# z and v projected in 512 columns for four token blocks at once, and the scan's decay tiles issued early

## The chip, the cores and the metric

The kernel runs on one core of a Trainium2 chip. The metric is the device time of one execution in microseconds (us). The engines of the core are TensorE (PE in the profile; its weight loads, which overlap the matmuls, are listed apart as PEld), VectorE (DVE), ScalarE (ACT), GpSimd (POOL) and SyncE (SP, whose queue issues the transfers). They run side by side, each in its own order, and wait for one another by semaphores.

## The reference

One layer of a decoder for one sequence of 512 tokens and 1024 features, all in float32: half a SwiGLU feed-forward, a mixer, and another half SwiGLU feed-forward, each added to x. The mixer projects the normed x once and gives the columns to two groups of heads. Cut to what matters here:

```python
proj = h @ w_in[l]                               # h = rms_norm(x), (512, 1024)
z, xbc, dt_raw, q, k, v = jnp.split(proj, split_idx, axis=-1)
xbc = jax.nn.silu(causal_dwconv(xbc, conv_w[l], conv_b[l]))
xs, bm, cm = jnp.split(xbc, [SSD_WIDTH, SSD_WIDTH + SSD_GROUPS * SSD_STATE], axis=-1)
...
a_cs = jnp.cumsum(dt * a.reshape(g, hg), axis=2)             # within a chunk of 128 tokens
xdt = xs * dt[..., None]
seg = a_cs[:, :, :, None] - a_cs[:, :, None, :]
decay = jnp.where(causal, jnp.exp(jnp.where(causal, seg, 0.0)), 0.0)
cb = jnp.einsum("bcign,bcjgn->bcijg", cm, bm)
y_diag = jnp.einsum("bcijgh,bcjghp->bcighp", cb[..., None] * decay, xdt)
... # states handed from chunk to chunk
y = y_diag + y_off + xs * d_skip
...
gated = (y_ssd * jax.nn.silu(z)).reshape(bsz, s, SSD_GROUPS, SSD_WIDTH // SSD_GROUPS)
y_ssd = rms_norm(gated, ssd_norm_w).reshape(bsz, s, SSD_WIDTH)
o = diff_attention(q, k, v, lam)                 # and a norm per head
x = x + concat([y_ssd, o]) @ w_out[l]
```

z and v are 1024 columns wide each; the scan has two groups of eight heads and four chunks of 128 tokens.

## The kernel before, in words

**The products.** Every float32 product of a projection is made of three matmuls: both operands are split into a high and a low part, and high x high, high x low and low x high are added up in PSUM, the memory into which PE writes. The normed x lies as `nm.xh` and `nm.xl` with the features on the partitions, in eight contraction blocks (`KD`) of 128.

**The weights.** They come in a fixed list of pieces of 128 x 1024 (`mixp`, L83 on). SP loads a piece into one of three `raw` tiles (`load_raw`), ACT casts it to the high part `whi` (L109), DVE subtracts to get the low part `wlo` (L110). `piece()` hands over the next one and has two more prepared ahead.

**The stages.** The first feed-forward takes until about 350 us. Then the columns xbc are projected and convolved (to about 440): `conv_tile` ends with a Silu on ACT (L467), `conv_tr` turns each result to tokens on the partitions with four transposes (`xt`, L474) and a copy (L476). Then come z and v, interleaved with the scan (440 to 570), then q and k with the attention (to about 755), the output projection and the second feed-forward.

**z and v before.** `tok_proj` projects 256 columns at a time: it takes two pieces of four contraction blocks, and for each of the four token blocks j runs 24 matmuls of 256 columns (lines L592 to L594). Two token blocks share one PSUM bank, from the pool behind `pJ`. It is a generator that yields after each token block; such a part is a unit. When a half is done, `cb` empties the bank. For z that is (`hr` holds half of the norm's factor of each token)

```python
S.activation(th, ps[:, jj, :], AF.Tanh, scale=hr[:, j:j + 1])
S.activation(zr, ps[:, jj, :], AF.Copy, scale=hr[:, j:j + 1])
V.scalar_tensor_tensor(zr, th, 1.0, zr, op0=ALU.add, op1=ALU.mult)
```

which is silu(z) = h (1 + tanh h) with h = z/2, on lines L608 to L610; for v it is a scaled copy (L617).

**The scan.** It has eight steps (c, g). `ssd_a` prepares one: a broadcast load of the decay sums from DRAM into the tile `ab` (L628), the product `cb` on PE and its masked copy `cbm` on DVE, then on ACT eight Relus (L634) and one Exp over 1024 columns (L635), on DVE `xdt`, the product `ab` x `cbm` (L639) and `xdd`, and on ACT eight scaled slices for `y` (L646). `ssd_o` takes the state on (L658 to L667), `ssd_d` makes the diagonal products `pd` (L676: eight matmuls of plain float32, each of which the profile shows as two) and multiplies with `sz`. `ssd_n` norms a group over its four chunks (L690), `ssd_c` transposes the result (`yt`, L697) and stores it. The tiles `ab`, `cbm`, `xdt` and `y` come from a pool `sb`, which is opened after the convolution's pool was closed and lies in the same memory.

**What sets the order.** A scheduler of the framework decides in which order each engine gets its instructions, from the program's order and its own estimates; the loop over the steps calls `unit()` between the parts of the scan, which is how projection lands between them. ScalarE loads a table of functions (L635 ACT_TABLE_LOAD) when the next function isn't in the table it holds; Silu and Exp are not in the same one here.

Of the kernel before, what the change touches and what calls it, by code (L numbers as in the profile page):

```python
# [8 lines left out]
F32 = mybir.dt.float32  # L9
# [3 lines left out]
AF = mybir.ActivationFunctionType  # L13
ALU = mybir.AluOpType
# [4 lines left out]
P = 128  # L19
T = 512  # L20
NB = T // P
KD = 8
# [16 lines left out]
def hymba_layer(ctx: ExitStack, tc: tile.TileContext, xT, gu1, dn1, wxbc, wdt, wz, wv, wqk,  # L39
                wo, gu2, dn2, cols, rows, out):  # L40
    nc = tc.nc
    V, S, G, PE = nc.vector, nc.scalar, nc.gpsimd, nc.tensor
# [6 lines left out]
    def pM(name, dt=F32):  # L49
        return pspool.tile([P, T], dt, tag="P", name=name)  # L50

    pJ = pP = pM
# [31 lines left out]
    mixp = [(wxbc[t], 1024) for t in (8, 9, 10, 11)]  # L84
    mixp += [(wdt, 128)]
    mixp += [(wxbc[t], 1024) for t in range(8)]
    for w, g in ((wz, 0), (wz, 1), (wv, 0), (wz, 2), (wz, 3), (wv, 1), (wv, 2), (wv, 3)):
        mixp += [(w[g, i], 1024) for i in range(2)]
    mixp += [(wqk[h, i], 1024) for h in range(8) for i in range(2)]
    for ds in ((0, 1), (2, 3), (4, 5)):  # L90
        mixp += [(wo[d, 0], 1024) for d in ds] + [(wo[d, 1, :, 0:512], 512) for d in ds]
# [7 lines left out]

    def load_raw(src, n):  # L100
        raw = wpool.tile([P, 1024], F32, tag="raw", name="raw", bufs=3)
        nc.sync.dma_start(raw[:, :n], src)
        return raw

    def split_part(raw, hi, lo, a, b):
# [14 lines left out]
    def prep(upto):  # L120
        while len(ready) < min(upto, len(pieces)):
            i = len(ready)
            if pieces[i][0] == "plain":
                _, src, n = pieces[i]
                ready.append(split_w(load_raw(src, n), n))
                continue
            r1, r2 = load_raw(pieces[i][1], 1024), load_raw(pieces[i][2], 1024)
            b11, b21, b12, b22 = r1[:, :512], r1[:, 512:], r2[:, :512], r2[:, 512:]
            n = scratch["n"]
            t = scratch["t"][:, n % 2] if n > 1 else scratch["hp"].tile([P, 2048], F32, tag="hp", name="tw0")  # L130
            scratch["n"] += 1
            t1, t3, t2, t4 = (t[:, q * 512:(q + 1) * 512] for q in range(4))
            V.tensor_sub(t1, b12, b11)
            V.tensor_sub(t3, b22, b12)
            V.tensor_sub(t2, b22, t1)
            V.tensor_sub(t4, t2, b21)
            ready.append([split_w(r1, 1024), split_w(t[:, :1024], 1024), split_w(t[:, 1024:], 1024),
                          split_w(b22, 512)])

    def piece(ahead=2):  # L140
        i = taken[0]
        taken[0] += 1
        prep(i + 1 + ahead)
        return ready[i]

    def blk(w, k, width=P):
        return w[:, k * width:(k + 1) * width]
# [25 lines left out]
    triu = const.tile([P, P], F32, name="triu")  # L173
# [219 lines left out]
    nm = [None]  # L393
# [8 lines left out]
    nm = nm[0]  # L402
# [7 lines left out]
    vt = [mix.tile([P, NB, 256], F32, tag=f"v{g}", name=f"v{g}") for g in range(4)]  # L410
# [22 lines left out]
    ssd = ssd_cm.__enter__()  # L433
    xs = ssd.tile([P, NB, 1024], F32, name="xs")
    sz = ssd.tile([P, NB, 1024], F32, name="sz")
    bT = ssd.tile([P, 2, T], F32, name="bT")
    cT = ssd.tile([P, 2, T], F32, name="cT")
    btok = ssd.tile([P, NB, 2, P], F32, name="btok")
    dts = ssd.tile([P, NB, 16], F32, name="dts")
    acs = ssd.tile([P, NB, 16], F32, name="acs")  # L440
# [3 lines left out]
    acs_d = dram.tile([64, P], F32, name="acs_d")  # L444
# [99 lines left out]
    for n, pair in enumerate(order):  # L544
# [3 lines left out]
        ps = [pP(f"xbc{n}{i}") for i in range(2)]  # L548
# [9 lines left out]
        for i in range(2):  # L558
            w = piece()
# [14 lines left out]
    hr = const.tile([P, NB], F32, name="hr")  # L574
# [4 lines left out]
    def tok_proj(name, cb, ahead=2):  # L579

        ws = [piece(ahead), piece(ahead)]
        for half in range(2):
            ps = pJ(f"{name}_{half}")
            psv = ps.rearrange("p (b c) -> p b c", c=256)
            for jj in range(2):
                j = half * 2 + jj
                o = psv[:, jj, :]
                for k in range(KD):
                    w = ws[k // 4]
                    hi, lo = blk(w[0], k % 4, 256), blk(w[1], k % 4, 256)  # L590
                    xh, xl = nm.xh[:, k, j * P:(j + 1) * P], nm.xl[:, k, j * P:(j + 1) * P]
                    PE.matmul(o, lhsT=xh, rhs=hi, start=k == 0, stop=False)  # L592
                    PE.matmul(o, lhsT=xh, rhs=lo, start=False, stop=False)  # L593
                    PE.matmul(o, lhsT=xl, rhs=hi, start=False, stop=k == KD - 1)  # L594
                if jj == 1:
                    cb(half, psv)
                yield
# [1 line left out]
    state = ssd.tile([P, 2, T], F32, name="state")  # L599
    sview = lambda a: a.rearrange("p (a b) -> p a b", b=64)  # L600

    def z_group(g):
        def cb(half, ps):
            for jj in range(2):
                j = half * 2 + jj
                zr = sz[:, j, g * 256:(g + 1) * 256]
                th = sb.tile([P, 256], F32, tag="th", name="th")
                S.activation(th, ps[:, jj, :], AF.Tanh, scale=hr[:, j:j + 1])  # L608
                S.activation(zr, ps[:, jj, :], AF.Copy, scale=hr[:, j:j + 1])
                V.scalar_tensor_tensor(zr, th, 1.0, zr, op0=ALU.add, op1=ALU.mult)  # L610
        return tok_proj(f"z{g}", cb)

    def v_group(g):
        def cb(half, ps):
            for jj in range(2):
                j = half * 2 + jj
                S.activation(vt[g][:, j, :], ps[:, jj, :], AF.Copy, scale=nm.r[:, j:j + 1])  # L617
        return tok_proj(f"v{g}", cb)

    ssq = [ssd.tile([P, NB], F32, name=f"ssq{g}") for g in range(2)]  # L620

    def ssd_a(c, g):

        hs = slice(g * 8, g * 8 + 8)
        sh = [P, 8, 64]
        cs = slice(c * P, (c + 1) * P)
        ab = sb.tile([P, 8, P], F32, tag="ab", name="ab", bufs=3)
        nc.sync.dma_start(ab, acs_d[c * 16 + g * 8:c * 16 + g * 8 + 8, :].partition_broadcast(P))  # L628
        pcb = pM(f"cb{c}{g}")
        PE.matmul(pcb[:, :P], lhsT=bT[:, g, cs], rhs=cT[:, g, cs], start=True, stop=True)  # L630
        cbm = sb.tile([P, P], F32, tag="cbm", name="cbm")
        V.tensor_mul(cbm, pcb[:, :P], triu)
        for h in range(8):
            S.activation(ab[:, h, :], ab[:, h, :], AF.Relu, bias=acs[:, c, g * 8 + h:g * 8 + h + 1], scale=-1.0)  # L634
        S.activation(ab, ab, AF.Exp, scale=-1.0)  # L635
        xg = sview(xs[:, c, g * 512:(g + 1) * 512])
        xdt = sb.tile(sh, F32, tag="xdt", name="xdt")
        V.tensor_tensor(xdt, xg, dts[:, c, hs].unsqueeze(2).to_broadcast(sh), op=ALU.mult)
        V.tensor_tensor(ab, ab, cbm.unsqueeze(1).to_broadcast([P, 8, P]), op=ALU.mult)  # L639
        xdd = None  # L640
        if c < NB - 1:
            xdd = sb.tile(sh, F32, tag="xdd", name="xdd", bufs=1)
            V.tensor_tensor(xdd, xdt, dsd[:, c, hs].unsqueeze(2).to_broadcast(sh), op=ALU.mult)
        y = sb.tile(sh, F32, tag="y", name="y")
        for h in range(8):
            S.activation(y[:, h, :], xg[:, h, :], AF.Copy, scale=row[:, R_DS + g * 8 + h:R_DS + g * 8 + h + 1])  # L646
        return ab, xdt, xdd, y

# [50 lines left out]
        nc.sync.dma_start(ysave[:, g * 4:g * 4 + 4, c, :], yt)  # L699

    steps = [(c, g) for g in range(2) for c in range(NB)]
    units = [z_group(0), z_group(1), v_group(0), z_group(2), z_group(3), v_group(1), v_group(2), v_group(3)]

    def unit(n=1):

        while n and units:
            try:
                next(units[0])
                n -= 1
            except StopIteration:  # L710
                units.pop(0)

    unit()
    for t, dst in last_conv:
        conv_tr(t, dst)
# [2 lines left out]
    sb = sb_cm.__enter__()  # L718
    unit()
    ops = ssd_a(*steps[0])  # L720
    unit(2)
    for n, s in enumerate(steps):
        ssd_o(*s, *ops)
        unit()
        nxt = ssd_a(*steps[n + 1]) if n < 7 else None
        unit()
        ssd_d(*s, *ops)
        ops = nxt
        if s[0] == NB - 1:
            ssd_n(s[1])  # L730
        if n in (5, 6):
            for c in (0, 1) if n == 5 else (2, 3):
                ssd_c(c, 0)
        unit()
# [324 lines left out]
```

## Time and profile before

| what | value |
|---|---|
| median of 3 runs | 1178.77 us (1178.4 to 1179.59) |
| own time of the profiled execution | 1178.91 us |
| its span in the profile | 1177.2 us |
| mean granted clock of PE over the span | 0.993 |
| PE busy | 1163.6 us |
| DVE busy | 854.4 us |
| ACT busy | 546.0 us |

All rows of this document are from that one profiled execution; its own time is 1.7 us more than its span, since the span begins with the first recorded instruction. A start in the rows is in us from there. Matmuls overlap in the engine, so the time that one of them costs is read from the distance of two starts, not from its own duration.

### The profile page before, as it was taken

How to read it: one execution, taken by the hardware profiler on the slowest of the kernel's cores; microseconds unless marked ns; L12 is line 12 of the kernel's file. 1: busy time of each engine (PE TensorE's matmuls, PEld its weight loads, DVE VectorE, ACT ScalarE, POOL GpSimd, SP SyncE). 2: the span in 40 equal slices, each digit the busy share in tenths (PEclk: the TensorE clock that was granted, in tenths of full speed). 3: DMA queues.
4: the chain of work that ended last, by engine and by line, in shares of the span. 5: the costliest groups of instructions: out<-in, count | busy, mean ns of one | idle time of the engine just before them, and what ended most of it. 6: DMA issues, size and time to landing. Idle time of an engine off the chain costs nothing.

```text
span 1177.2 us, 18641 instructions
## 1 busy us (share of the span) xinstructions
PE 1163.6 (99%) x7435; PEld 1026.4 (87%) x7435; DVE 854.4 (73%) x1509; ACT 546.0 (46%) x938; POOL 36.0 (3%) x63
## 2 busy tenths in 40 slices
PE   8999999999999998999999999999999999999998
PEld 6789999999888788999988887688889999999986
DVE  6887877877768974685477877436798888777763
ACT  5443343433344458794465656334354443334331
POOL 1000000000013000000000000013000000000000
PEclk9999999999999998999999999899999999999999
DMA  7323333333245223323421204144222333333332
GB/s 234 90 64 98 94 102 109 112 95 112 79 134 197 73 89 126 108 83 112 130 73 36 67 25 130 33 161 127 71 79 92 115 114 95 103 108 99 105 103 85
DMA packets 42391, 119.53 MB, mean 102 GB/s; under 512 B 4608, under 2 KB 9920, under 8 KB 42304
## 3 DMA queue, kind: packets, MB, share of 16 engines
q1 hardware_dynamic: 41024, 114.15, 31.6%
q0 software_dynamic: 1280, 4.20, 1.0%
q8 instruction: 58, 0.95, 0.3%
q14 instruction: 29, 0.24, 0.1%
HBM read 112.00 MB, written 6.32 MB: 101 GB/s over the span
## 4 chain that ended last, share of the span: by engine, by line
PE 97%; ACT 1%; DMA 0%; DVE 0%; SPq 0%; issue 0%; POOL 0%
PE s L308 10%; PE s L306 10%; PE s L307 10%; PE dn L153 7%; PE dn L152 7%; PE dn L151 7%; PE gu L151 3%; PE gu L152 3%; PE gu L153 3%; PE qk L592 3%; PE wo L151 3%; PE wo L152 3%; PE wo L153 3%; PE qk L594 3%; PE qk L593 3%; PE sc L801 2%
## 5 line engine op out<-in xcount | busy, mean ns | idle before, releaser
L109 ACT CAST whi<-raw 128x1024 fp32r<-128x1024 f32 (+2 forms) x217 | 189.5, 875 | 316.9 <-PE s L307 123.1
L110 DVE TENSOR_TENSOR wlo<-raw,whi 128x1024 fp32r<-128x1024 f32 (+3 forms) x225 | 223.0, 993 | 127.6 <-ACT whi L109 121.7
L307 PE MATMUL s<-al,whi 128*128 128x256 f32 x952 | 266.4, 281 | 0.0
L306 PE MATMUL s<-ah,whi 128*128 128x256 f32 x952 | 265.4, 281 | 0.0
L308 PE MATMUL s<-ah,wlo 128*128 128x256 f32 x952 | 264.8, 281 | 0.0
L307 PEld LDWEIGHTS s<-al,whi 128*128 128x128 f32 x952 | 179.3, 188 | 2.2
L306 PEld LDWEIGHTS s<-ah,whi 128*128 128x128 f32 x952 | 178.8, 188 | 2.3
L308 PEld LDWEIGHTS s<-ah,wlo 128*128 128x128 f32 x952 | 178.3, 188 | 0.1
L152 PE MATMUL dn<-h,whi 128*128 128x512 f32 x352 | 139.0, 395 | 0.0
L153 PE MATMUL dn<-h,wlo 128*128 128x512 f32 x352 | 138.7, 395 | 0.0
L151 PE MATMUL dn<-h,whi 128*128 128x512 f32 x352 | 137.9, 395 | 0.0
L109 ACT CAST whi<-tw 128x1024 fp32r<-128x1024 f32 x68 | 70.3, 1050 | 144.0 <-PE s L307 64.9
L110 DVE TENSOR_TENSOR wlo<-tw,whi 128x1024 fp32r<-128x1024 f32 x68 | 81.9, 1217 | 3.0 <-ACT whi L109 2.9
L153 PEld LDWEIGHTS dn<-h,wlo 128*128 128x128 f32 x352 | 66.1, 188 | 15.0
L151 PEld LDWEIGHTS dn<-h,whi 128*128 128x128 f32 x352 | 66.1, 188 | 14.3
L152 PEld LDWEIGHTS dn<-h,whi 128*128 128x128 f32 x352 | 66.2, 188 | 13.7
L592 PE MATMUL qk<-whi,xhm 128*128 128x256 f32 x256 | 74.2, 290 | 0.0
L594 PE MATMUL qk<-whi,xlm 128*128 128x256 f32 x256 | 71.9, 281 | 0.0
L593 PE MATMUL qk<-wlo,xhm 128*128 128x256 f32 x256 | 71.7, 280 | 0.0
L342 DVE SCALAR_TENSOR_TENSOR x<-dn,x 128x512 f32<-128x512 f32 x64 | 44.0, 687 | 37.3 <-PE dn L153 36.3
L151 PE MATMUL gu<-xh,whi 128*128 128x512 f32 x160 | 64.9, 406 | 2.1 <-POOL whi L107 2.0
L152 PE MATMUL gu<-xl,whi 128*128 128x512 f32 x160 | 63.6, 398 | 0.0
(274 smaller groups left out, 2248.9 us busy)
## 6 DMA issues: line engine op xcount, KB each, us to landing
raw<-in_gu SPq DMA_DIRECT2D x86, 512.0 KB, 3.6
raw<-in_dn SPq DMA_DIRECT2D x48, 384.0 KB, 3.2
raw<-in_wqk SPq DMA_DIRECT2D x16, 512.0 KB, 3.6
raw<-in_wxbc SPq DMA_DIRECT2D x12, 512.0 KB, 3.7
raw<-in_wo SPq DMA_DIRECT2D x10, 512.0 KB, 3.7
raw<-in_dn SPq DMA_DIRECT2D x16, 256.0 KB, 2.7
raw<-in_wz SPq DMA_DIRECT2D x8, 512.0 KB, 3.6
raw<-in_wv SPq DMA_DIRECT2D x8, 512.0 KB, 3.6
```

What stands on the lines that cost most here:

```text
L109: S.copy(hi[:, a:b], raw[:, a:b])
L110: V.tensor_sub(lo[:, a:b], raw[:, a:b], hi[:, a:b].bitcast(F32))
L151: PE.matmul(ps, lhsT=hi, rhs=xh, start=start, stop=False)
L152: PE.matmul(ps, lhsT=hi, rhs=xl, start=False, stop=False)
L153: PE.matmul(ps, lhsT=lo, rhs=xh, start=False, stop=stop)
L306: PE.matmul(ps, lhsT=hi, rhs=ah[:, i, a], start=i == 0, stop=False)
L307: PE.matmul(ps, lhsT=hi, rhs=al[:, i, a], start=False, stop=False)
L308: PE.matmul(ps, lhsT=lo, rhs=ah[:, i, a], start=False, stop=i == 3)
L342: V.scalar_tensor_tensor(x[d], ps, 0.5, x[d], op0=ALU.mult, op1=ALU.add)
L592: PE.matmul(o, lhsT=xh, rhs=hi, start=k == 0, stop=False)
L593: PE.matmul(o, lhsT=xh, rhs=lo, start=False, stop=False)
L594: PE.matmul(o, lhsT=xl, rhs=hi, start=False, stop=k == KD - 1)
```

## The change

Four things change in the stretch from about 440 to 570 us.

*Wider groups.* `tok_pair` takes the place of `tok_proj` for z and v: a matmul has 512 columns, two groups of 256. A piece now holds two contraction blocks of both groups, so its `raw` tile is filled by two transfers of 256 KB, and the operand of a matmul is two runs of 256 columns, 512 apart. All four token blocks are worked on with each piece, in four PSUM banks that are held from the first piece to the fourth. q and k still use `tok_proj`.

*z's activation.* The Tanh is written in place into PSUM; Copy goes first, and DVE reads the Tanh from PSUM. The tile `th` is gone.

*The decay tile.* `ssd_ab` is cut out of `ssd_a`; `ab` and `cbm` come from the longer-lived pool `ssd`, and the first decay tile is issued ahead of the first unit. The exp table is loaded by an instruction of its own ahead of that.

*ScalarE's order.* `tc.issue_after` pins the Relus and the Exp of each decay tile behind the Exp of the one before (the first behind the table load), and the slices for `y` behind the Exp of their own step.

```diff
@@ -84,8 +84,9 @@
-    for w, g in ((wz, 0), (wz, 1), (wv, 0), (wz, 2), (wz, 3), (wv, 1), (wv, 2), (wv, 3)):
-        mixp += [(w[g, i], 1024) for i in range(2)]
+    for w in (wz, wv):
+        for g in (0, 2):
+            mixp += [(tuple(w[g + b, i, :, c:c + 512] for b in range(2)), 1024) for i in range(2) for c in (0, 512)]
...
@@ -99,7 +100,10 @@
-        nc.sync.dma_start(raw[:, :n], src)
+        parts = src if isinstance(src, tuple) else (src,)
+        m = n // len(parts)
+        for q, part in enumerate(parts):
+            nc.sync.dma_start(raw[:, q * m:(q + 1) * m], part)
...
@@ -599,50 +603,78 @@
-    def z_group(g):
...
-    def v_group(g):
...
+    def tok_pair(name, cb):
+
+        ps = [None] * NB
+        for q in range(4):
+            w = [z.rearrange("p (g k c) -> p k g c", g=2, k=2) for z in piece()]
+            for half in range(2):
+                for j in (2 * half, 2 * half + 1):
+                    if q == 0:
+                        ps[j] = pJ(f"{name}_{j}")
+                    o = ps[j].rearrange("p (g c) -> p g c", g=2)
+                    for kk in range(2):
+                        k = 2 * q + kk
+                        xh, xl = nm.xh[:, k, j * P:(j + 1) * P], nm.xl[:, k, j * P:(j + 1) * P]
+                        PE.matmul(o, lhsT=xh, rhs=w[0][:, kk], start=k == 0, stop=False)
+                        PE.matmul(o, lhsT=xh, rhs=w[1][:, kk], start=False, stop=False)
+                        PE.matmul(o, lhsT=xl, rhs=w[0][:, kk], start=False, stop=k == KD - 1)
+                    if q == 3:
+                        cb(j, ps[j])
+                yield
+
+    def z_pair(g):
+        def cb(j, ps):
+            zr = sz[:, j, g * 512:(g + 1) * 512]
+            S.activation(zr, ps, AF.Copy, scale=hr[:, j:j + 1])
+            S.activation(ps, ps, AF.Tanh, scale=hr[:, j:j + 1])
+            V.scalar_tensor_tensor(zr, ps, 1.0, zr, op0=ALU.add, op1=ALU.mult)
+        return tok_pair(f"z{g}", cb)
+
+    def v_pair(g):
+        def cb(j, ps):
+            for b in range(2):
+                S.activation(vt[2 * g + b][:, j, :], ps[:, b * 256:(b + 1) * 256], AF.Copy, scale=nm.r[:, j:j + 1])
+        return tok_pair(f"v{g}", cb)
...
+    def ssd_ab(c, g):
+
+        cs = slice(c * P, (c + 1) * P)
+        ab = ssd.tile([P, 8, P], F32, tag="ab", name="ab", bufs=3)
+        nc.sync.dma_start(ab, acs_d[c * 16 + g * 8:c * 16 + g * 8 + 8, :].partition_broadcast(P))
...
+        cbm = cbms[c, g] = ssd.tile([P, P], F32, tag="cbm", name="cbm", bufs=2)
+        V.tensor_mul(cbm, pcb[:, :P], triu)
+        with tc.issue_after(pinned[0]):
+            for h in range(8):
+                S.activation(ab[:, h, :], ab[:, h, :], AF.Relu, bias=acs[:, c, g * 8 + h:g * 8 + h + 1], scale=-1.0)
+            e = S.activation(ab, ab, AF.Exp, scale=-1.0)
+        pinned[0] = e.ins
+        return ab, e.ins
 
     def ssd_a(c, g):
...
+        ab, y_after = abs_.pop((c, g)) if (c, g) in abs_ else ssd_ab(c, g)
...
+        with tc.issue_after(y_after):
+          for h in range(8):
             S.activation(y[:, h, :], xg[:, h, :], AF.Copy, scale=row[:, R_DS + g * 8 + h:R_DS + g * 8 + h + 1])
         return ab, xdt, xdd, y
...
@@ -699,7 +731,7 @@
-    units = [z_group(0), z_group(1), v_group(0), z_group(2), z_group(3), v_group(1), v_group(2), v_group(3)]
+    units = [z_pair(0), z_pair(1), v_pair(0), v_pair(1)]
...
@@ -710,6 +742,8 @@
+    pinned[0] = tc.keep_in_program_order(S.preload_act_table_set("exp_and_others")).ins
+    abs_[steps[0]] = ssd_ab(*steps[0])
     unit()
...
@@ -718,7 +752,7 @@
     unit()
     ops = ssd_a(*steps[0])
-    unit(2)
+    unit(4)
```

The scheduler turns this into the following orders; numbers at a name tell one buffer from another.

ScalarE between the convolution and the first Exp, before. `ab_4241` is the first decay tile, `ab_4368` the second, `y_` the slices, `th_` and `sz_` belong to z, `whi_` is a weight cast:

```order
L634 ACTIVATE ab_4241<-ab_4241,acs_3495 128x128 x8
L109 CAST whi_4333<-raw_4331 128x1024
L634 ACTIVATE ab_4368<-ab_4368,acs_3495 128x128 x3
L608 ACTIVATE th_4319<-z0_1_4270,hr_4149 128x256
L609 ACTIVATE sz_3490<-z0_1_4270,hr_4149 128x256
L608 ACTIVATE th_4323<-z0_1_4270,hr_4149 128x256
L609 ACTIVATE sz_3490<-z0_1_4270,hr_4149 128x256
L667 COPY state_4153<-st00_4328 128x512
L109 CAST whi_4339<-raw_4337 128x1024
L634 ACTIVATE ab_4368<-ab_4368,acs_3495 128x128 x3
L635 ACT_TABLE_LOAD
L635 ACTIVATE ab_4241<-ab_4241 128x1024
```

ScalarE in the changed kernel, from the convolution's last Silu (L471) on. `ab_4159` is the first decay tile, `ab_4330` the second, `xt6` and `xt7` the last two transposes of the convolution:

```order
L471 ACTIVATE xst_4149<-a_4144 128x512
L745 ACT_TABLE_LOAD
L656 ACTIVATE ab_4159<-ab_4159,acs_3495 128x128 x8
L480 COPY xs_3489<-xt6_4195 128x4x128
L657 ACTIVATE ab_4159<-ab_4159 128x1024
L656 ACTIVATE ab_4330<-ab_4330,acs_3495 128x128 x8
L480 COPY xs_3489<-xt7_4201 128x4x128
L678 ACTIVATE y_4230<-xs_3489,row_3476 128x64 x8
L113 CAST whi_4273<-raw_4270 128x1024
L657 ACTIVATE ab_4330<-ab_4330 128x1024
L678 ACTIVATE y_4350<-xs_3489,row_3476 128x64 x8
L656 ACTIVATE ab_4433<-ab_4433,acs_3495 128x128
```

The table load, the Relus and the Exp of the first tile now stand directly behind the last Silu, and the slices for `y` behind the Exp of their step. Before, the first Exp stood behind z's activations and parts of the second tile's Relus.

The queue of SP, before. `acs_d` is the DRAM copy of the decay sums, the loads on L628 fill the decay tiles, those on L102 the weight pieces:

```order
L540 DMA acs_d_3499<-acsT_3926 64x128
L102 DMA raw_4162<-in_wz 128x1024
L102 DMA raw_4331<-in_wv 128x1024
L102 DMA raw_4337<-in_wv 128x1024
L102 DMA raw_4536<-in_wz 128x1024
L628 DMA ab_4241<-acs_d_3499 128x1024
L628 DMA ab_4368<-acs_d_3499 128x1024
```

and in the changed kernel:

```order
L106 DMA raw_4174<-in_wz 128x512 x2
L544 DMA acs_d_3499<-acsT_3926 64x128
L649 DMA ab_4159<-acs_d_3499 128x1024
L649 DMA ab_4330<-acs_d_3499 128x1024
L649 DMA ab_4433<-acs_d_3499 128x1024
L106 DMA raw_4239<-in_wz 128x512 x2
```

The three decay loads (now L649) moved up past three pieces of v and one of z, to a place right behind the store.

PE at the first `pd`, in the changed kernel (L708). `z0_3` is the fourth token block of the first pair, `z1_0` the first of the second pair:

```order
L619 MATMUL z0_3_4218<-whi_4242,xhm_3280 128x512
L620 MATMUL z0_3_4218<-wlo_4243,xhm_3280 128x512
L621 MATMUL z0_3_4218<-whi_4242,xlm_3281 128x512
L708 MATMUL pd000_4301<-xdt_4225,ab_4159 128x64 x8
L619 MATMUL z1_0_4395<-whi_4273,xhm_3280 128x512
L620 MATMUL z1_0_4395<-wlo_4274,xhm_3280 128x512
L621 MATMUL z1_0_4395<-whi_4273,xlm_3281 128x512
L619 MATMUL z1_0_4395<-whi_4273,xhm_3280 128x512
L620 MATMUL z1_0_4395<-wlo_4274,xhm_3280 128x512
L621 MATMUL z1_0_4395<-whi_4273,xlm_3281 128x512
L619 MATMUL z1_1_4402<-whi_4273,xhm_3280 128x512
```

The bank of `z1_1` is the second that the next pair asks for, six matmuls behind the eight of `pd`. Before, `pd` stood behind 144 matmuls of 256 columns, now behind 96 of 512.

## Rows read from the trace of the kernel before

**Rows 1.** The page's part 1: busy us, share of the span, instructions.

```profile
PE 1163.6 (99%) x7435; PEld 1026.4 (87%) x7435; DVE 854.4 (73%) x1509; ACT 546.0 (46%) x938; POOL 36.0 (3%) x63
```

**Rows 2.** The waits of PE, whole run: us in total, times, longest.

```profile
PE pd L676 <- DVE ab L639: 4.7, 1, 4.7
...
PE at L825 <- DVE nmx L808: 1.2, 1, 1.2
```

**Rows 3.** Windows: length, busy us of PE to POOL, PE clock, DMA share, GB/s.

```profile
450.00:500.00 50.00, 45.31 (x331) 42.23 (x330) 28.61 (x41) 39.88 (x108) 0.00 (x0) 0.93 0.36 113
700.00:750.00 50.00, 48.80 (x276) 36.40 (x275) 34.79 (x93) 30.11 (x72) 0.00 (x0) 0.94 0.29 90
```

**Rows 4.** A window of 4 us, the same columns.

```profile
464.00:468.00 4.00, 4.00 (x21) 4.00 (x22) 1.78 (x4) 4.00 (x12) 0.00 (x0) 0.54 0.00 0
```

**Rows 5.** The timeline of PE: start, duration, instruction, [idle before, releaser].

```profile
458.85 0.28 PE L594 MATMUL z<-whi,xlm 128*128 128x256 f32 x1
463.82 3.21 PE L676 MATMUL pd<-xdt,ab 128*128 128x64 f32 x16 [4.69 <-DVE ab L639]
466.79 0.56 PE L592 MATMUL z<-whi,xhm 128*128 128x256 f32 x1
...
471.20 0.28 PE L594 MATMUL z<-whi,xlm 128*128 128x256 f32 x1
...
479.25 1.89 PE L676 MATMUL pd<-xdt,ab 128*128 128x64 f32 x16
480.95 0.36 PE L592 MATMUL v<-whi,xhm 128*128 128x256 f32 x1
481.15 0.28 PE L593 MATMUL v<-wlo,xhm 128*128 128x256 f32 x1
```

**Rows 6.** The chain that ended last, 446 to 475: start, us, what.

```profile
448.68 2.64 ACT y L646 x12
...
452.42 2.16 ACT ab L634 x7
454.57 0.94 ACT whi L109
...
456.40 0.36 ACT th L608
...
457.84 0.47 ACT state L667
...
460.16 1.28 ACT L635
461.45 1.06 ACT ab L635
462.54 1.24 DVE ab L639
```

**Rows 7.** The waits of SP's queue, 420 to 610.

```profile
SPq L628 <- PE xt L474: 4.6, 1, 4.6
```

**Rows 8.** The timeline of ACT at the convolution's last Silu.

```profile
444.44 0.64 ACT L467 ACTIVATE xst<-a 128x512 f32<-128x512 f32 x1
```

**Rows 9.** The timeline of PE: xbc (46 steps) and z (27 steps).

```profile
428.10 0.40 PE L152 MATMUL xbc<-xlm,whi 128*128 128x512 f32 x1
...
438.83 0.39 PE L153 MATMUL xbc<-xhm,wlo 128*128 128x512 f32 x1
...
440.05 0.28 PE L593 MATMUL z<-wlo,xhm 128*128 128x256 f32 x1
...
443.20 0.28 PE L593 MATMUL z<-wlo,xhm 128*128 128x256 f32 x1
```

**Rows 10.** The page's part 5: group | busy, mean ns | idle before.

```profile
L342 DVE SCALAR_TENSOR_TENSOR x<-dn,x 128x512 f32<-128x512 f32 x64 | 44.0, 687 | 37.3 <-PE dn L153 36.3
```

**Rows 11.** The timelines of DVE and PE at the end of the scan.

```profile
560.28 2.74 DVE L690 SCALAR_TENSOR_TENSOR sz<-sz,ssr,row 128x512 f32<-128x512 f32 x4
...
569.61 0.60 PE L697 MATMUL yt<-ident,sz 128*128 128x128 f32 x4
```

More of the change, by code (lines that the diff above doesn't have):

```diff
@@ L600, in hymba_layer @@
     sview = lambda a: a.rearrange("p (a b) -> p a b", b=64)
-    def z_group(g):
[L603 to L611, printed above, removed]
@@ L613, in v_group @@
-    def v_group(g):
[L614 to L618, printed above, removed]
-    ssq = [ssd.tile([P, NB], F32, name=f"ssq{g}") for g in range(2)]
+    def tok_pair(name, cb):
[16 more added lines that the diff above has]
+                yield
@@ new lines, in hymba_layer @@
+    ssq = [ssd.tile([P, NB], F32, name=f"ssq{g}") for g in range(2)]
+    abs_, cbms = {}, {}
+    pinned = [None]
+    def ssd_ab(c, g):
+        cs = slice(c * P, (c + 1) * P)
+        ab = ssd.tile([P, 8, P], F32, tag="ab", name="ab", bufs=3)
+        nc.sync.dma_start(ab, acs_d[c * 16 + g * 8:c * 16 + g * 8 + 8, :].partition_broadcast(P))
+        pcb = pM(f"cb{c}{g}")
+        PE.matmul(pcb[:, :P], lhsT=bT[:, g, cs], rhs=cT[:, g, cs], start=True, stop=True)
+        cbm = cbms[c, g] = ssd.tile([P, P], F32, tag="cbm", name="cbm", bufs=2)
[6 more added lines that the diff above has]
+        return ab, e.ins
@@ L626, in ssd_a @@
         cs = slice(c * P, (c + 1) * P)
[L627 to L635, printed above, removed]
+        ab, y_after = abs_.pop((c, g)) if (c, g) in abs_ else ssd_ab(c, g)
         xg = sview(xs[:, c, g * 512:(g + 1) * 512])
@@ L638, in ssd_a @@
         V.tensor_tensor(xdt, xg, dts[:, c, hs].unsqueeze(2).to_broadcast(sh), op=ALU.mult)
-        V.tensor_tensor(ab, ab, cbm.unsqueeze(1).to_broadcast([P, 8, P]), op=ALU.mult)
+        V.tensor_tensor(ab, ab, cbms.pop((c, g)).unsqueeze(1).to_broadcast([P, 8, P]), op=ALU.mult)
         xdd = None
@@ L644, in ssd_a @@
         y = sb.tile(sh, F32, tag="y", name="y")
-        for h in range(8):
+        with tc.issue_after(y_after):
+          for h in range(8):
             S.activation(y[:, h, :], xg[:, h, :], AF.Copy, scale=row[:, R_DS + g * 8 + h:R_DS + g * 8 + h + 1])
```

## The prediction

> **What bounds the kernel now.** I read the page's busy shares first: TensorE (PE) is busy 1163.6 of 1177.2 us [rows 1]. Only two things can then make the kernel faster: less time per matmul, or the few microseconds in which PE waits or runs at its lower clock. The waits of PE come next. The longest in the whole run is 4.7 us, by the diagonal products `pd` of the scan (L676), for the product `ab` of VectorE (DVE); near the end of attention there is one of 1.2 us [rows 2]. The windows of 50 us say the same and add the clock: the one from 450 has 45.31 busy us at a mean granted clock of 0.93, the one from 700 a clock of 0.94 [rows 3]. A finer window shows what follows the idle: from 464 to 468 PE is busy all the time, at 0.54, so most of it runs at the lower of its two levels, 1.2 GHz [rows 4].
>
> What the stall costs comes from the starts of PE's instructions [rows 5]. The last z matmul before it starts at 458.85 and `pd` at 463.82, 4.97 apart, where a 256-column matmul holds PE for 0.1167 (below): 4.85 lost. After it the eight `pd` products take 463.82 to 466.79 = 2.97 us, the next chunk's 479.25 to 480.95 = 1.70: 1.27 lost. Then 20 steps of 256-column matmuls take 466.79 to 471.20 = 4.41 us; at full clock they are 20 x 0.1167 (below) and 0.08 more for the first behind `pd`, which starts its successor after 0.20 in the next chunk, so 2.42: 1.99 lost. **Stall and slow stretch together: 4.85 + 1.27 + 1.99 = 8.11 us.**
>
> Why `pd` waited is in the chain that ended last [rows 6]. From 448.7 to 462.5 it lies on ScalarE (ACT), which hardly idles there: it scales fifteen slices for `y`, only then begins the Relus of the first decay tile, weaves in casts, Relus of the next tile, z's activations and the state copy, and at 460.16 loads the exp table (1.28) for the first Exp; DVE's product follows, and PE starts. Part of it begins earlier: the SP queue held the decay loads for 4.6 us, behind the convolution's last transposes `xt`, which still read the memory where the decay tiles lie [rows 7].
>
> **The change, part by part.**
>
> *The first decay tile is early.* Its tiles now live in the long-lived pool; the order of the SP queue puts the three loads right behind the store of `acs`, ahead of the fourth z piece. ACT issues table load, eight Relus and Exp directly behind the convolution's last Silu, which before ran 444.44 to 445.08 [rows 8]; with 0.3 for the `cbm` product now ahead of it on DVE (my guess), 445.4. Prices from the chain [rows 6]: load 1.28, a Relu 2.16/7 = 0.31, an Exp 1.06, and for the copy that stands between them, 512 columns out of PSUM, the state copy's 0.47. Exp of step 0 ends at 445.4 + 1.28 + 2.47 + 0.47 + 1.06 = 450.7. DVE then needs its small products and the 1.24 of `ab` [rows 6]: about 453.
>
> When does PE ask for it? Before, from the second z matmul at 440.05 [rows 9] to one spacing after the last at 458.85 [rows 5] lay 143 of 256 columns, 16.7 us, and 2.2 us of transposes, state product and `cb`. Now 96 of 512 columns stand there, 22.4 us, and the same 2.2: `pd` comes due at about 464.6, with its input ready since 453. The 11 us between are what hides this edit; were they gone, each us that the tile is late would be paid again. The stall and its slow stretch go: **-8.11 us.**
>
> *512 columns instead of 256.* 768 matmuls become 384. The 512-column convolution projection starts one each (438.83 - 428.10)/46 = 0.2333 us, z's 256-column ones (443.20 - 440.05)/27 = 0.1167 [rows 9]: twice the latter is the former. Starts are printed to 0.01, so at most 1 ns per matmul can hide in that, 0.4 us in all; I take 0. The operand is now two runs of 256 columns, which no row has. Bounds: one run of 512 at 0.2333, and two whole matmuls of 256, also 0.2333; I take 0 again.
>
> The Trainium skill, page "TensorE: Matmul & The Clock Gate", section "Back-to-back issue gap", gives a warm matmul a fixed 2.5 ns beside its columns. By it the 384 fewer would save 0.96 us (an estimate from that page), and the sum would be -9.1; the rows just read do not show that part.
>
> *Four token blocks at once, two contraction blocks a piece.* Each piece still serves 24 x 0.2333 = 5.6 us of PE, as before. But a pair now keeps four PSUM banks until its end, so the next pair's banks come free only through ACT and DVE. This is where a stall could arise next, so I followed ACT to there. Behind 450.7, by the chain's prices [rows 6]: eight Relus 2.47, copy 0.47, eight `y` slices at 2.64/12 = 0.22, 1.76, a cast 0.94, Exp 1.06, `y` 1.76, Relus with two casts 4.35, state copy 0.47: 464.0. Then Copy and Tanh of block 0, 512 columns each. No row has them in place in PSUM; the state copy of 512 from PSUM takes 0.47, two of the old 256-column ones 2 x 0.36 = 0.72. I take 0.47, the same width: 464.9; DVE's scalar_tensor_tensor from PSUM, 0.69 [rows 10], makes 465.6. PE asks for the second bank of the next pair after `pd` (1.70) and six matmuls (1.40): 467.7. Margin 2.1 us, or 1.6 with the dearer end. The later boundaries have more: the next z drains start behind an idle ACT (it waits there for decay loads whose buffer the `pd` two steps earlier frees), and v's drains have one operation less per column. Queued behind such a wait on ACT are casts for pieces that PE needs over 15 us later, so it costs nothing; with that cover gone it would cost one for one.
>
> The page "ScalarE: Activation LUTs" of the Trainium skill, section "What ACT_TABLE_LOAD costs", adds a drain of 1.38 us to each switch; here the Exp starts 0.01 after the load of 1.28 ends [rows 6], so the trace does not show it. By that page the margin would be 0.7 (an estimate), still no stall.
>
> *The rest.* SP issues 16 more loads of half the size, hidden in a queue that waits for free buffers. ACT does 16 operations of 0.47 for z in place of 32 of 0.36, DVE 8 of 0.69 for 16 smaller ones; neither bounds. Between the last `pd` and the last transposes `yt` PE has 144 matmuls of 256 columns before, 16.8 us, and now 36 wide and 24 narrow ones, 11.2 us, so `yt` is asked for 5.6 us sooner after `pd`. What it needs first, the first of four norm products, was done at 560.28 + 2.74/4 = 560.97, 8.6 us before it was asked for at 569.61 [rows 11]. Cover 3.0 us: cost 0.
>
> **Sum:** own time of the profiled execution 1178.91 - 8.11 = 1170.80. That execution stands 0.14 above the median of 1178.77, so I forecast 1170.7 us.
>
> **Rivals.**
> 1. *The bank wait appears.* ACT is later than worked out by more than the 1.6 to 2.1 of margin, and PE waits at the first boundary. For: ACT is loaded without a gap for 20 us, and the added Tanh in place is unseen. Against: all other prices are rows. Idle of 1 to 4 us at full clock: 1171.7 to 1174.7.
> 2. *The same wait, longer: not faster.* If ACT's order holds the drains back so far that PE idles and its clock falls as at 464, the price is the idle and 1.27 + 1.99 = 3.26; from 4.85 us of idle on, ACT being 6.5 to 7.0 us late, nothing is gained, and with 9 us of idle the time is 1170.7 + 9 + 3.26 = 1183.
> 3. *Two runs cost more than one.* From 8.11/384 = 21 ns per matmul on it eats the gain; at 40 ns the time is 1186. The Trainium skill's page "PSUM — Partial Sum Buffer", section "Specifications (TRN2)", says non-contiguous access slows matmuls significantly; the output here is contiguous, only the moving operand is not. Against it: two whole 256-column matmuls already cost no more than one of 512 [rows 9].
> 4. *The other slow stretch changes.* A clock of 0.94 over 50 us costs 3.0 us [rows 3]. The wait there is only 1.2 us [rows 2]; with the scan ending earlier, it may fall differently: 1167.7.
> 5. *Matmuls do have a fixed part* beside their columns: up to 0.4 us by the rows, 1170.3. The page on TensorE would give 1169.7 by its 2.5 ns.
>
> **How the numbers follow.** Forecast (1170.7, give or take 1) 0.62; rival 1 0.15; rival 2 0.06; rival 3 0.04; rival 4 0.08; rival 5 0.05. A difference under 0.2% (2.4 us) cannot be told from none here: faster means below 1176.4. The cases but rivals 2 and 3 lie there, less 0.01 of rival 1: 0.89 faster. Rivals 2 and 3 begin at no gain, and with that 0.01 give 0.05 same and 0.06 slower. The range takes in rivals 4 and 1: 1167.3 to 1175.3, leaving out about 0.12. The likeliest case alone: 1169.7 to 1171.7.
>
> **What would show it.** PE's wait by `pd` for `ab` is gone, and the window from 450 has 50 busy us at clock 1.00. The 512-column z matmuls start every 0.2333 us. The last scan transposes, at 569.61 before [rows 11], start at about 561.5. ACT's Copy and Tanh of block 0 start near 464, and PE waits for no `sz`. Attention, from there on, looks as before, 8.1 us earlier. I am wrong if the first z matmuls of the second pair wait for DVE or ACT, if their spacing is over 0.24, or if the gain by 569 is lost again by 800.

## The result and the profile after

The changed kernel takes 1168.78 us in the median (1167.5 to 1173.2 over four runs), the kernel before 1178.63 us in the same comparison; the ratio is 0.9925 with an interval of 0.9911 to 0.9939, so 7 to 10.5 us less. The forecast was 1170.7 us. The profiled execution took 1168.65 us at a span of 1166.9, 10.3 us less than the span of before.

The page's part 1 of the kernel after, in the order of [rows 1]:

```profile
PE 1158.3 (99%) x7051; PEld 1004.0 (86%) x7051; DVE 854.2 (73%) x1501; ACT 543.5 (47%) x922; POOL 36.1 (3%) x63
```

The waits of PE over the whole run (us in total, times, longest) no longer name `pd`; the one near the end of attention is there as before [rows 2]. `gu` is the first product of the first feed-forward.

```profile
PE gu L155 <- DVE acc L232: 1.7, 1, 1.7
PE warm L167 <- DVE zeros L164: 1.3, 1, 1.3
PE at L859 <- DVE nmx L842: 1.2, 1, 1.2
PE psdtT L499 <- ACT dtr L496: 0.7, 1, 0.7
```

The windows of 50 us, with the columns of [rows 3]. The first is now full at full clock, the second is as it was:

```profile
450.00:500.00 50.00, 50.00 (x244) 39.93 (x243) 33.46 (x45) 42.23 (x110) 0.00 (x0) 1.00 0.33 106
700.00:750.00 50.00, 48.79 (x233) 35.05 (x233) 32.13 (x77) 27.89 (x62) 0.00 (x0) 0.93 0.31 95
```

The timeline of PE (start, duration, instruction): the end of the convolution's projection and the first pair of z, the first `pd`, and the last transposes of the scan, which answer to [rows 5, 9, 11]. A count at the edge of a queried window covers only what lies in it; the last transposes are sixteen in both kernels:

```profile
436.93 0.39 PE L157 MATMUL xbc<-xhm,wlo 128*128 128x512 f32 x1
...
438.95 0.40 PE L619 MATMUL z<-whi,xhm 128*128 128x512 f32 x1
439.19 0.39 PE L620 MATMUL z<-wlo,xhm 128*128 128x512 f32 x1
...
448.45 0.40 PE L619 MATMUL z<-whi,xhm 128*128 128x512 f32 x1
...
455.45 0.39 PE L619 MATMUL z<-whi,xhm 128*128 128x512 f32 x1
...
462.37 0.40 PE L621 MATMUL z<-whi,xlm 128*128 128x512 f32 x1
462.60 1.89 PE L708 MATMUL pd<-xdt,ab 128*128 128x64 f32 x16
464.31 0.48 PE L619 MATMUL z<-whi,xhm 128*128 128x512 f32 x1
464.62 0.40 PE L620 MATMUL z<-wlo,xhm 128*128 128x512 f32 x1
...
559.30 0.82 PE L729 MATMUL yt<-ident,sz 128*128 128x128 f32 x6
```

Three things are to be seen. Behind the last z matmul `pd` starts after 0.23 us, the time of one matmul of 512 columns, and its eight products take 464.31 - 462.60 = 1.71 us, as undisturbed ones did before. Two neighbours of 512 columns in two runs start 0.24 us apart (438.95, 439.19), and over the 30 steps from 448.45 to 455.45 it is 7.00/30 = 0.2333. And the stretch from the start of the last `xbc` matmul to the start of the last transposes `yt` takes 559.30 - 436.93 = 122.37 us, where before it took 569.61 - 438.83 = 130.78. **This stretch is worth 8.41 us.** Of the other 1.9 us of the spans, all lie ahead of it: the last `xbc` matmul starts at 436.93 instead of 438.83. Behind it nothing is left: from the last `yt` to the last matmul it is 603.57 and 603.55 us.

ACT's timeline from the convolution's last Silu (L471) on shows the early tile, and the first block's Copy and Tanh; DVE's shows the product that `pd` waits for (L670) and the first product out of PSUM (L631):

```profile
442.29 0.64 ACT L471 ACTIVATE xst<-a 128x512 f32<-128x512 f32 x1 [2.62 <-DVE a L466]
442.94 1.28 ACT L745 ACT_TABLE_LOAD   x1
444.24 2.45 ACT L656 ACTIVATE ab<-ab,acs 128x128 f32<-128x128 f32 x8
446.60 0.56 ACT L480 COPY xs<-xt 128x512 f32<-128x512 f32 x1
447.06 1.06 ACT L657 ACTIVATE ab<-ab 128x1024 f32<-128x1024 f32 x1
...
461.27 0.69 ACT L629 ACTIVATE sz<-z,hr 128x512 f32<-128x512 f32 x1
461.86 0.64 ACT L630 ACTIVATE z<-z,hr 128x512 f32<-128x512 f32 x1
462.42 0.68 ACT L629 ACTIVATE sz<-z,hr 128x512 f32<-128x512 f32 x1
```

```profile
449.82 1.22 DVE L670 TENSOR_TENSOR ab<-ab,cbm 128x1024 f32<-128x1024 f32 x1
...
462.61 0.68 DVE L631 SCALAR_TENSOR_TENSOR sz<-z,sz 128x512 f32<-128x512 f32 x1
```

`ab` is ready at 449.82 + 1.22 = 451.04 and asked for at 462.60: 11.6 us of cover. From start to start the first Copy takes 0.59 us and the first Tanh in place 0.56.

### The profile page after: what moved, and what is told of

Same layout as the page of the kernel before. It is cut to its first block, busy times and chain, and to the rows that moved or that the text cites. A ratio compares the mean times of both kernels' runs of the same rounds, so it can differ in the third digit from the quotient of the medians.

```text
span 1166.9 us, 17871 instructions
## 1 busy us (share of the span) xinstructions
PE 1158.3 (99%) x7051; PEld 1004.0 (86%) x7051; DVE 854.2 (73%) x1501; ACT 543.5 (47%) x922; POOL 36.1 (3%) x63
## 4 chain that ended last, share of the span: by engine, by line
PE 99%; DVE 0%; DMA 0%; SPq 0%; ACT 0%; issue 0%
PE s L312 10%; PE s L310 10%; PE s L311 10%; PE dn L157 7%; PE dn L156 7%; PE dn L155 7%; PE gu L155 3%; PE gu L157 3%; PE gu L156 3%; PE qk L596 3%; PE wo L155 3%; PE wo L156 3%; PE wo L157 3%; PE qk L598 3%; PE qk L597 3%; PE sc L835 2%
## 5 line engine op out<-in xcount | busy, mean ns | idle before, releaser
L157 PE MATMUL gu<-xh,wlo 128*128 128x512 f32 x160 | 62.9, 393 | 0.0
```

What stands on the lines that cost most here:

```text
L157: PE.matmul(ps, lhsT=lo, rhs=xh, start=False, stop=stop)
```

## The experiments

Each is compared with the kernel before by the ratio of its runs. Beside it stands the stretch from the last `xbc` matmul to the last `yt` in its profile, with the two starts that it lies between. It repeats to 0.02 us between profiles of one kernel unless the clock differs: 130.78 and 130.76 in two profiles of the kernel before, 122.37 and 122.38 in two of the change.

| kernel | ratio to before (95% interval) | stretch, us | from and to, us |
|---|---|---|---|
| before | 1 | 130.78 | 438.83, 569.61 |
| before, second profile | | 130.76 | 436.59, 567.35 |
| before, third profile | | 131.29 | 440.39, 571.68 |
| the full change | 0.9925 (0.9911 to 0.9939) | 122.37 | 436.93, 559.30 |
| the full change again | 0.9924 (0.9910 to 0.9937) | 122.38 | 436.25, 558.63 |
| wide pairs alone | 0.9923 (0.9912 to 0.9935) | 123.17 | 436.89, 560.06 |
| early tile alone | 0.9910 (0.9895 to 0.9924) | 122.66 | 439.69, 562.35 |
| before with two more units ahead | 0.9934 (0.9916 to 0.9952) | 122.66 | 438.41, 561.07 |
| one run of 512 columns | 0.9914 (0.9901 to 0.9927) | 122.37 | 437.19, 559.56 |
| without the table load ahead | 0.9989 (0.9979 to 0.9999) | 130.70 | 440.09, 570.79 |
| without both pins | 0.9990 (0.9980 to 0.9999) | 130.26 | 438.72, 568.98 |
| without the pin of `y` | 0.9929 (0.9911 to 0.9947) | 122.37 | 438.22, 560.59 |
| five more matmuls at the start | 0.9921 (0.9908 to 0.9934) | 122.37 | 439.36, 561.73 |

**Theory A** is the prediction's: the early decay tile removes the stall and the slow stretch behind it, and the width is worth nothing. **Rival B:** half as many matmuls are what is gained.

### The wide pairs alone

`tok_pair`, `z_pair`, `v_pair`, the new list of pieces and the line `unit(4)` of the change's diff (`unit(2)` before) stay, and `ssd_a` is put back as it was before. Against the full change:

```diff
-    def ssd_ab(c, g):
...
     def ssd_a(c, g):
...
-        ab, y_after = abs_.pop((c, g)) if (c, g) in abs_ else ssd_ab(c, g)
+        ab = sb.tile([P, 8, P], F32, tag="ab", name="ab", bufs=3)
...
-    pinned[0] = tc.keep_in_program_order(S.preload_act_table_set("exp_and_others")).ins
-    abs_[steps[0]] = ssd_ab(*steps[0])
```

> The 512-column pairs for z and v alone; the decay tiles, the table load and the order of ScalarE are left as they were before the change. Theory A (the gain is the stall at the first pd and the slow stretch behind it; width is worth nothing): the stall is back. By the order of ScalarE the first Exp stands behind sixteen y slices, sixteen Relus and two casts and ends near 464, VectorE's product near 465.5, while PE asks at 462.6: some 3 us of idle and up to 3.3 us of lower clock behind it, so 1174 to 1178 us, at most 4 us better than before. Rival B (the gain comes from half as many matmuls): 1167 to 1171, as the full change.

Measured: ratio 0.9923, median 1170.34 us. Theory A is wrong here, and the time is the one that rival B gave. But the profile doesn't show faster matmuls, it shows the wait by `pd` shrunk to half a microsecond. The waits of PE, then ACT's timeline (slices, table load, first Exp, first Copy of z), DVE's product `ab` and PE's `pd`:

```profile
PE pd L696 <- DVE ab L659: 0.5, 1, 0.5
```

```profile
448.17 3.93 ACT L666 ACTIVATE y<-xs,row 128x64 f32<-128x64 f32 x16
...
459.58 1.28 ACT L655 ACT_TABLE_LOAD   x1
460.88 1.06 ACT L655 ACTIVATE ab<-ab 128x1024 f32<-128x1024 f32 x1
...
464.73 0.67 ACT L629 ACTIVATE sz<-z,hr 128x512 f32<-128x512 f32 x1
```

```profile
461.97 1.23 DVE L659 TENSOR_TENSOR ab<-ab,cbm 128x1024 f32<-128x1024 f32 x1 [1.70 <-ACT ab L655]
```

```profile
463.25 2.00 PE L696 MATMUL pd<-xdt,ab 128*128 128x64 f32 x16 [0.52 <-DVE ab L659]
```

The first Exp starts 23.99 us behind the last `xbc` matmul (460.88 - 436.89); before it was 22.62 (461.45 - 438.83) [rows 6, 9], so the tile is not earlier but 1.4 us later. PE asks later: the idle began 20.30 us behind the last `xbc` matmul before (459.13 - 438.83) [rows 5, 9] and begins 25.84 behind it now (463.25 - 0.52 - 436.89). In front of the first `pd` stand 96 matmuls of 512 columns, 22.4 us, where 144 of 256, 16.8 us, stood before. That is a matter of units, not of width: a unit is 24 matmuls of 256 columns or 12 of 512, 2.8 us either way, and six of them stood there before, eight now, because of `unit(4)`. Theory A had this side right (PE asks at 462.6; measured 463.25 - 0.52 = 462.73); what it had wrong is the product, which it put at 465.5 and which was ready at 461.97 + 1.23 = 463.20. Behind the half microsecond that is left the clock from 450 to 500 stays at 1.00, and the stretch is 123.17 us, 0.80 more than with the full change.

### The early tile alone

The hunks on `ssd_ab`, `ssd_a` and the two lines ahead of the first unit, put into the kernel before; z and v stay in groups of 256 columns, and `unit(2)` stays too:

```diff
+    pinned[0] = tc.keep_in_program_order(S.preload_act_table_set("exp_and_others")).ins
+    abs_[steps[0]] = ssd_ab(*steps[0])
     unit()
     for t, dst in last_conv:
...
     ops = ssd_a(*steps[0])
     unit(2)
```

> The early decay tile in the long-lived pool, the table load and the pinned order, with z and v in 256-column groups as before. Theory A: PE no longer waits at the first pd, 50 busy us in the window from 450 at clock 1.00, and the time is that of the full change within 0.2%: 1167 to 1172 us. Rival B: the gain mostly stays out, 1175 or more. Rival C (both parts are needed, because the narrow groups' drains now stand behind the Relus and Exp): a new wait of PE for z's drain, 1172 to 1176.

Measured: ratio 0.9910, median 1169.67 us; theory A holds. No wait by `pd`, the window from 450 full at clock 1.00, and `ab` ready at 453.84, 6.0 us before `pd` starts. The window, DVE's product and PE's `pd`:

```profile
450.00:500.00 50.00, 50.00 (x401) 47.13 (x400) 33.67 (x51) 45.18 (x126) 0.00 (x0) 1.00 0.33 105
```

```profile
452.61 1.23 DVE L650 TENSOR_TENSOR ab<-ab,cbm 128x1024 f32<-128x1024 f32 x1 [0.53 <-ACT ab L637]
```

```profile
459.83 0.44 PE L688 MATMUL pd<-xdt,ab 128*128 128x64 f32 x3
```

The stretch is 122.66: 8.12 us less than before, where the prediction's sum was 8.11. Rival C's wait for z's drain is not there.

### Two more units ahead, in the kernel before

> The kernel before with one number changed: four units of projection instead of two stand ahead of the first step of the scan (48 more narrow matmuls, 5.6 us, ahead of the first pd); groups of 256 columns, late decay tile, ScalarE's order not pinned. Theory D (the stall is a matter of how much projection PE has in front of the first pd; wide pairs removed it by putting 96 x 512 in place of 144 x 256 there, not by their width): PE asks for the product at about 464.7 in the times of the first profile, it is ready at about 463.7, so no wait or one under 0.5 us, no slow stretch, and the time falls by 7.6 to 8.4 us below the kernel before. Rival (the added units' drains on ScalarE push the first Exp back by as much): the wait stays above 2 us and the time within 3 us of before.

```diff
     ops = ssd_a(*steps[0])
-    unit(2)
+    unit(4)
```

Measured: ratio 0.9934, median 1171.67 us. Theory D holds: this one number in the kernel before, with narrow groups, a late tile and no order pinned, gives 8.12 us of the stretch. DVE's `ab` is ready at 463.17 and PE's `pd` starts at 464.15 with no wait, 0.98 us later:

```profile
461.94 1.23 DVE L639 TENSOR_TENSOR ab<-ab,cbm 128x1024 f32<-128x1024 f32 x1 [1.62 <-ACT ab L635]
```

```profile
464.15 1.11 PE L676 MATMUL pd<-xdt,ab 128*128 128x64 f32 x9
```

So there are two independent ways out of the same stall, an earlier tile and more projection in front, and the change has both: its diff turns this same `unit(2)` into `unit(4)`, which the four things listed under "The change" do not name. The pairs cannot do without a number above 2 there: a pair empties its first bank only in its seventh unit (`q == 3`), and with `unit(2)` the first step would use z behind the sixth.

### One run of 512 columns

```diff
-            nc.sync.dma_start(raw[:, q * m:(q + 1) * m], part)
+            if len(parts) == 2:
+                nc.sync.dma_start(raw.rearrange("p (k g c) -> p k g c", g=2, k=2)[:, :, q, :], part.rearrange("p (k c) -> p k c", k=2))
...
-            w = [z.rearrange("p (g k c) -> p k g c", g=2, k=2) for z in piece()]
+            w = [z.rearrange("p (k n) -> p k n", k=2) for z in piece()]
```

> The full change, but the two loads of a piece interleave the two groups in the raw tile, so that a matmul's moving operand is one run of 512 columns instead of two runs of 256. Theory A (two runs cost nothing): the same as the full change within 0.2%, starts 0.2333 us apart. Rival (two runs cost something that is hidden in rows of 0.01): up to 1 us faster. Rival on the loads (rows of 1 KB in place of 2 KB): the loads land later, but nothing waits for them.

Measured: ratio 0.9914, and the stretch is 122.37 us, the same to 0.01. The two runs cost nothing that the profile shows; 0.01 us over 384 matmuls is under 0.03 ns each.

### The change once more, and the kernel before twice more

> The changed kernel once more. Of the 10.3 us by which the two profiled spans differ, 1.9 lie in the first 25 us, where both kernels do the same. Theory A: this part is chance of the execution (a wait of 1.7 instead of 2.0 us and, with the longer one, a lower clock behind it), so it shows in some profiles and not in others, whichever kernel runs; the scan is worth 8.4 and the median ratio is near 0.9925. Rival: the start is faster in every execution with the change, and the ratio is 0.991 to 0.992.

> The kernel before, one more profile. Theory A (the 1.9 us in the first 25 us are chance): the first transposed row sum of the norm (psr) starts between 24.5 and 28.5, not always near 27.25, and the span differs from the first profile by what this start differs. Rival: 27 or later again, as in the first profile of this kernel, while the profiles with wide pairs had 24.7 to 25.6.

> The same once more: a third profile of the kernel before, for the spread of the start, with the same two expectations.

Measured: the changed kernel again 0.9924. The start differs from execution to execution, as theory A had it: in the three profiles of the kernel before `psr`, PE's row sums of the first norm, starts at 27.25, 25.01 and 28.78 us, with spans of 1177.2, 1175.0 and 1179.3; in two of the change at 25.34 and 24.67. The third, 28.78, lies outside the 24.5 to 28.5 that was expected. What decides the start is not shown. Over all thirteen profiles it goes with the mean granted clock of the first 30 us: 24.67 to 25.63 in the five where that is 1.00 (one of before, four with wide pairs), 26.64 to 28.10 in the six at 0.94 (three with wide pairs), 28.51 and 28.78 in the two at 0.89. Three of these rows, of the kernel before (its second and its third profile; with the window from 450) and of the kernel without the pin of `y`:

```profile
0.00:30.00 30.00, 26.26 (x109) 19.13 (x110) 22.03 (x44) 16.09 (x23) 5.52 (x20) 1.00 0.73 239
450.00:500.00 50.00, 45.30 (x331) 42.23 (x330) 30.21 (x43) 39.97 (x107) 0.00 (x0) 0.93 0.29 98
```

```profile
0.00:30.00 30.00, 25.81 (x93) 18.26 (x94) 18.58 (x32) 16.15 (x23) 6.03 (x20) 0.89 0.71 227
450.00:500.00 50.00, 45.31 (x327) 42.23 (x326) 28.45 (x43) 39.95 (x108) 0.00 (x0) 0.90 0.33 109
```

```profile
0.00:30.00 30.00, 26.48 (x102) 19.07 (x103) 20.71 (x38) 16.08 (x23) 5.94 (x20) 0.94 0.73 231
```

So of the 10.3 us between the two first profiles 8.4 are the change's, and 1.9 are not. The ratio 0.9925 of 1178.63 is 8.8 us, with 8.4 well inside its interval. The third profile of before also shows that the stall's price isn't fixed: the same idle, but 0.90 instead of 0.93 from 450 to 500, and 0.5 us more.

### Without the table load, and without the pins

> The full change without the loading of the exp table by an instruction of its own and without the pin of the first decay tile behind it. The scheduler then puts the first three Exps between the convolution's Silus, with five more table loads on ScalarE. Theory A: ScalarE has idle time of 2 to 3 us before each Silu there, PE waits for none of them, and the time is that of the full change within 0.2%. Rival: the loads (1.28 us each) make the last Silus late, PE waits for the transposes of the convolution and its clock falls: 2 to 8 us slower than the full change.

```diff
-    pinned[0] = tc.keep_in_program_order(S.preload_act_table_set("exp_and_others")).ins
     abs_[steps[0]] = ssd_ab(*steps[0])
...
-        with tc.issue_after(pinned[0]):
+        with (tc.issue_after(pinned[0]) if pinned[0] else ExitStack()):
```

Measured: ratio 0.9989, median 1178.07 us: nearly all of the gain is gone, and theory A's expectation fell. The waits of PE, ACT's timeline (load and Exp of a decay tile, L657; load and Silu of the convolution, L471) and the window from 440:

```profile
PE xt L478 <- ACT xst L471: 5.3, 1, 5.3
```

```profile
431.02 1.28 ACT L657 ACT_TABLE_LOAD   x1
432.31 1.06 ACT L657 ACTIVATE ab<-ab 128x1024 f32<-128x1024 f32 x1
...
437.16 1.28 ACT L471 ACT_TABLE_LOAD   x1
438.45 0.63 ACT L471 ACTIVATE xst<-a 128x512 f32<-128x512 f32 x1
...
439.56 1.28 ACT L657 ACT_TABLE_LOAD   x1
440.85 1.06 ACT L657 ACTIVATE ab<-ab 128x1024 f32<-128x1024 f32 x1
...
444.26 1.28 ACT L471 ACT_TABLE_LOAD   x1
445.56 0.63 ACT L471 ACTIVATE xst<-a 128x512 f32<-128x512 f32 x1
```

```profile
440.00:450.00 10.00, 4.68 (x19) 3.82 (x18) 4.26 (x6) 9.93 (x16) 0.00 (x0) 0.77 0.11 40
```

The Exps have moved between the Silus, and each of the three Exps that stand there brings two loads of 1.28 us, its own and the next Silu's. ACT is full (9.93 of 10 us), the last Silus come late, and PE waits 5.3 us for `xt`, with its clock at 0.77 in that window. The stretch is 130.70, 8.33 more than with the load: the stall is back under another name. The edit takes away the first tile's pin too, which hangs on the load.

> The full change with the table load kept where it is, but without either pin: the scheduler again puts the first three Exps between the convolution's Silus. Theory E (what the early tile needs is the pin that keeps its Exp behind the last Silu; the table load by itself keeps nothing in place): as without the load, a wait of PE of about 5 us for the convolution's last transposes and a lower clock behind it, 1175 to 1180 us. Rival (the load alone is enough, since the scheduler puts Exps behind it): as the full change, 1168 to 1171.

```diff
-        with tc.issue_after(pinned[0]):
+        if True:
...
-        with tc.issue_after(y_after):
+        if True:
```

Measured: ratio 0.9990, median 1178.06 us. Theory E holds: with the load but without the pins PE waits 5.5 us for `xt` in two pieces. The load alone keeps nothing in place. Whether the pin would do without the load, behind another instruction, was not run.

```profile
PE xt L478 <- ACT xst L471: 5.5, 2, 4.1
```

> The full change without the pin of the y slices behind the Exp of their step; load and pin of Relus and Exps stay. In ScalarE's order eight slices move by a few places, none ahead of the first Exp. Theory E: the second decay tile is at most 1 us later, it has several us in hand, and the time is that of the full change within 0.2%. Rival: the slices hold the second Exp or a bank's drain up and PE waits: 1 us or more slower, with a wait by name in the profile.

```diff
-        with tc.issue_after(y_after):
+        if True:
```

Measured: ratio 0.9929, stretch 122.37: the pin of `y` does nothing here, as theory E had it. So of the two pins it is that of the Relus and Exps which holds the gain.

### Five more matmuls at the start

> The full change with five more matmuls on zeros (as the warming ones ahead of the first product) behind the first three matmuls of the first feed-forward, where PE waits 1.7 to 3.5 us for its next operands in all profiles. Theory F (what differs between executions at the start is whether PE's clock falls after that wait): the wait is about 1.1 us shorter, the clock from 0 to 30 us stays at 1.00, the norm's first row sum (psr) starts at 24.5 to 25.7, and the median is 0 to 1.5 us below that of the full change. Rival (the start differs by when its transfers land): psr spreads from 24.7 to 28.8 as before and the median is the same.

```diff
     def mm3(ps, w, k, xh, xl, start, stop):
...
+        if not filled:
+            filled.append(pP("fill"))
+            for i in range(5):
+                PE.matmul(filled[0], lhsT=zeros[:, :P], rhs=zeros, start=i == 0, stop=i == 4)
```

A miss. The new matmuls waited themselves, for a PSUM bank that DVE still read, so they ran behind the idle time instead of in it:

```profile
PE fill L163 <- DVE acc L238: 1.7, 1, 1.7
```

The clock of the first 30 us is 0.94, `psr` starts at 27.75, and the ratio, 0.9921, is that of the change. Whether PE's clock can be held up there stays open.

## Why the prediction was right, and where its reasons were too narrow

**The price of the stall was right.** The sum gave 8.11 us; the early tile alone gives 8.12 in the stretch, the full change 8.41. The walk through the stretch holds too, if the 1.9 us of the start are added to the measured times: `ab` ready at 452.9 (predicted about 453), `pd` due at 464.5 (464.6), last `yt` at 561.2 (561.5). Attention is as before, moved by a constant: rival 4 did not happen.

**The step that was too narrow is who gets the credit.** The prediction put the whole gain down to "The first decay tile is early" and took 0 for "512 columns instead of 256", asking only what a matmul costs. The 5.6 us by which `pd` moves back stand in its own text, as part of the tile's cover; that they remove the stall without the tile (7.61 of 8.41 us by the wide pairs alone) was not worked out, nor that they come from `unit(4)` and not from the columns. The chain that ended last named ScalarE's order as the cause, and it was one; the wait had a second side, how soon PE asks.

**Width by itself** was right at about nothing. The early tile alone and the full change differ by 122.66 - 122.37 = 0.29 us, 0.8 ns for each of the 384 matmuls saved. It lies inside the prediction's bound of 0.4 us, but it also holds all else that comes with the pairs, so that width alone has this price is not shown. The Trainium skill, page "TensorE: Matmul & The Clock Gate", section "Back-to-back issue gap", gives an isolated warm matmul 2.5 ns beside its columns, by which the difference would be 0.96 us (an estimate); these rows show less than a third of that.

**The bank wait (rivals 1 and 2) did not come.** Copy of block 0 started at 461.27, which with the start's 1.9 us is 463.2 against 464.0 in the walk. Copy and Tanh were dearer than the 0.47 taken (0.59 and 0.56), within the dearer end of 0.72; DVE was done at 463.29, and PE's second bank, six matmuls behind 464.31, was due at 465.7: a margin of 2.4 us, predicted 1.6 to 2.1.

**Two runs (rival 3)** cost nothing that the profile shows (122.37 us with either).

**What the prediction left out** is the price of the order. It took the place of the table load and of the Exps from the changed kernel's order as given and named no cost if they were elsewhere. Without the load and the pin on it the stretch is 8.33 us longer, with the load but without the pins 7.89: the same early tile turns into a wait for the convolution. The cost of a change of table there is the load alone: 1.28 us, and the Exp starts 0.01 later (431.02, 432.31). The drain of 1.38 us that the Trainium skill's page "ScalarE: Activation LUTs", section "What ACT_TABLE_LOAD costs", adds to each is not in these rows either.

**The rest of the difference** is mostly not the change's. The profiled execution was forecast at 1170.80 and took 1168.65 us: 0.3 of the difference lies in the stretch, 1.9 in the start, which moved by up to 4.1 us between profiles (24.67 to 28.78). So the median of 1168.78 lies in the range, but below the 1169.7 to 1171.7 of the likeliest case. The prediction did not weigh the start, which can move an execution by more than the 2 us by which the forecast was off.

## What to carry to other kernels

A wait has two sides: before crediting an early producer, work out when the consumer would ask if only the other part of the change were made. Try the smallest line of a change by itself first; here `unit(4)` alone, in the kernel before, gave 8.12 of the 8.41 us. An operation that is moved ahead on an engine that switches function tables needs its order fixed, or a scheduler may put it between operations of the other table and pay a load each way.

## What was not expected of the hardware

PE's clock after a short wait at the start differs between executions of one kernel, and the length of the wait alone doesn't decide it: the mean of the first 30 us was 1.00 behind waits of 2.33, 2.73 and 2.93 us 0.94 behind waits of 2.00, 2.11 and 2.30, and 0.89 behind 2.78 and 2.85. The same idle of 4.69 us in the scan cost 8.1 us in two profiles and 8.6 in a third, as the granted clock from 450 to 500 was 0.93 or 0.90. And in the second profile of the change the part behind the last `yt` took 604.94 us instead of 603.57, with 0.90 instead of 0.93 from 700 to 750.
